# Two mixers of a two-block network: sixteen of their twenty-eight weight blocks multiplied in float32 straight from the loaded blocks

## The chip, the cores and the metric

The kernel runs on one core of one Trainium2 chip. A core has five engines with a program each: TensorE (PE in the profile, with its weight loads as PEld), VectorE (DVE), ScalarE (ACT), GpSimd (POOL) and SyncE (SP), which here issues the loads. The metric is the device time of one execution in microseconds (us), as the median of several runs; less is better.

## The reference, cut to what matters

A sequence of 256 tokens with 1024 features goes through two blocks of two layers each, everything in float32. The first block (attention, RWKV time mixing, two convolution FFNs) is not touched. Each layer of the second block begins with a mixer:

```python
def second_block(x, c, positions, ...):
    for l in range(DEPTH):                       # DEPTH = 2
        mod = jax.nn.silu(c) @ ada_w[l] + ada_b[l]
        sh1, sc1, g1, sh2, sc2, g2 = jnp.split(mod[:, None, :], 6, axis=-1)
        h = rmsnorm(x, ln1_g[l]) * (1.0 + sc1) + sh1
        z = h @ w_in[l]                          # 1024 -> 2560
        xr, yr, q, k, v = jnp.split(z, splits, axis=-1)
        lru = rg_lru(causal_conv(xr, conv_w[l], conv_b[l]), ...) * jax.nn.gelu(yr)
        att = diff_attention(q, k, v, positions, ...)
        x = x + g1 * (jnp.concatenate([lru, att], axis=-1) @ w_out[l])
        h = rmsnorm(x, ln2_g[l]) * (1.0 + sc2) + sh2
        f = swiglu(h, ...) if l % 2 == 0 else moe(h, ...)
        x = x + g2 * f
    return rmsnorm(x, final_g)
```

The attention has four heads, each the difference of two softmaxes of 64-wide queries and keys, followed by an rms norm of the head's output. The recurrence `rg_lru` has 512 channels, a convolution of four taps ahead of it and two gates from small block matrices.

## The kernel before, in words

**Layout and products.** Activations lie feature-major: eight tiles of 128 features x 256 tokens. All large weights are packed on the host into blocks of 128 x 1024 floats (512 KB) in the order of use. A block is either *split* or *raw*. For a split block ScalarE casts it to fp32r (`whi`, line 377) and VectorE or GpSimd subtracts that from the raw block (`wlo`, line 379). The activations have such parts too, `Ahi` and `Alo`. A product is then three fp32r matmuls, hi x hi, lo x hi and hi x lo (`mm3`, lines 595 to 597; token-major, for the values, lines 624 to 626). A raw block is multiplied as it is in float32; before the change only the first block of the network has such blocks.

**The stream.** `Stream` keeps two free lists, of raw buffers and of pairs for split blocks. `advance` issues loads on SyncE as long as there is a raw buffer, and splits as long as there is a pair; a split gives its raw buffer back when both parts are made, and a pair is free again when the next block is taken. In the first mixer there are ten raw buffers and five pairs, in the second fourteen and four. `k.st.share = 3` makes every third split of a mixer a GpSimd one, and splits are then given a priority of 60 over other work.

**A mixer** is `mixer2`, run with l = 0 and l = 1. Its steps are written in one list, `MIX_ORDER`:

```python
MIX_ORDER = "q0 x0 s0 q1 x1 s1 q2 v0 s2 t0 q3 v1 m0 s3 r0 n0 t1 y0 m1 t2 m2 n1 y1 t3 o0 n2 m3 o1 n3 o2 l0 l1 o3 l2 l3".split()
```

q (queries and keys of a head), x (the recurrence's input), v (values) and y (gate) take two blocks each, o and l (output rows for a head and for four feature tiles of the recurrence) one each: 28 blocks. s is scores and softmax, t the transposes of the softmax, m its product with the values, n the head's norm, r the recurrence. q0 and x0 run ahead of the norm's factors by token (`start`, results scaled by the row `frow`; `scaled`, line 1504, writes them to `gy` and `th`). After x0, `norm_split` makes the normed input for everything else: for each feature tile a product on VectorE (`nt`, line 573), `Ahi` on ScalarE (574) and `Alo` on VectorE (575). For l = 0 the residual h, which is still the result of the first block before its last norm, is multiplied by that norm's row and gain on GpSimd, two products for each of eight tiles (1544 and 1545). The row lies in the tile of the values, `V`.

The names that the steps use: `xc` the convolution (three products on VectorE for each feature tile, line 1562), `gates` its matmuls (1567), `rope_in`, `rope_sw` and `rope_out` the rotation of queries and keys (675, 683 to 685), `sc` the scores (1594, maximum 695, exponential 701, scaling 1597 to 1601), scores' matmuls 1592, transposes 1609 to `PT`, product with the values 1618, `sq` a square for the statistics (499, matmul 459), `rs` the factors by token (542, on GpSimd).

**What sets the order.** The program is written step by step as in the list, and a scheduler then orders each engine's instructions by priority (place in the program, less the bonus of the splits) and its own estimate of when their inputs are there. On the chip each engine takes its instructions strictly in that order.

**The stretches.** Mixer 1 has a start (q0, x0, with the residual of the layer before) to 818.4 us, a middle (the other sixteen blocks of q, x, v and y) from 818.4 to 902.1 and an out stage (o and l) to 927.2; then follows the FFN. Mixer 2 has them up to 1153.3, 1237.7 and 1262.8, then the routing and the experts to the end.

Of the kernel before, what the change touches and what calls it, by code (L numbers as in the profile page):

```python
# [10 lines left out]
F32 = mybir.dt.float32  # L11
# [3 lines left out]
AF = mybir.ActivationFunctionType  # L15
# [4 lines left out]
P = 128  # L20
T = 256
# [13 lines left out]
# ---------------------------------------------------------------- layout  # L35
# [53 lines left out]
def _const_arrays():  # L89
# [11 lines left out]
    # up to here for the first block only  # L101
# [19 lines left out]
def _colunit(w, c0, n=256):  # L121
    """columns c0:c0+n of a [1024, *] matrix as [128, 8*n], rows of one partition d = kt*128 + p"""
    return w[:, c0:c0 + n].reshape(-1, P, n).transpose(1, 0, 2).reshape(P, -1)


# steps of a mixer of block 2: queries and keys, scores, turned scores, values and output of the heads (q, s, t, m, o),
# the projections of values, recurrence and gate (v, x, y), the recurrence (r) and its output (l)
# [4 lines left out]
# the tokens and two more columns  # L132
# [7 lines left out]
def stream_units(inp):  # L140
    """blocks [128, 1024] of the streamed weights in the order of use; with inp None only their number"""
# [68 lines left out]
    for l in range(2):  # L210
        for c in MIX_ORDER:
            n, i = c[0], int(c[1:])
            if n == "q":
                add(2048, lambda: _colunit(np.concatenate([win[l][:, 1024 + i * P:1024 + (i + 1) * P], win[l][:, 1536 + i * P:1536 + (i + 1) * P]], 1), 0))
            elif n in MIX_COLS:
                add(2048, lambda: _colunit(win[l], MIX_COLS[n] + 256 * i))
# [57 lines left out]
class K:  # L274
    """state shared by the stages"""
# [15 lines left out]
# ---------------------------------------------------------------- weight stream  # L291
class Stream:
    """weights in the order of use: loads run ahead, then hi and lo parts but for the raw ones"""

    def __init__(self, k):
# [3 lines left out]
        # free memory for loads and for parts: what always stays, and what stays to the end of some phases  # L299
# [14 lines left out]
    def open(self, raw, spl, phases=1):  # L314
        """for the next phases: blocks to load and split blocks on top of those that stay"""
# [7 lines left out]
    def extend(self, more, upto=1):  # L323
        """more blocks to load, to the last one or up to one"""
# [35 lines left out]
    def _cuts(self, n):  # L360
        """the last blocks go in halves"""
# [27 lines left out]
    def after(self, n):  # L389
        """what follows on ScalarE comes after the split of the n-th block from here"""  # L390
        return self.k.tc.issue_after(self.ins[min(self.cur + n, self.nsplit - 1)])

    def done(self):
        """the parts handed out last are used"""
# [4 lines left out]
    def get(self):  # L399
        """the next block: its parts, or a raw one, kept until free()"""  # L400
# [10 lines left out]
    def free(self):  # L411
# [1723 lines left out]
```

## Time and profile before

| what | value |
|---|---|
| time, median of three runs | 2157.73 us (2155.24 to 2157.91) |
| span of the profiled execution | 2161.8 us |
| TensorE busy | 2060.4 us, 95% |
| VectorE busy | 1808.6 us, 84% |
| ScalarE busy | 1361.7 us, 63% |
| GpSimd busy | 302.8 us, 14% |
| two mixers, start to end of the out stages | 798.4 to 927.2 and 1137.2 to 1262.8 |

The span is that of one execution, taken by the profiler; it lies 4.1 us above the median of the runs. The busy time of a pipelined TensorE does not say that it is at its peak: the distance from one matmul's start to the next does, and so does the clock that the throttle granted, which the windows give as a share of 2.4 GHz (0.50 is 1.2 GHz). A float32 matmul shows as two records. A row of the waits says which instruction of another engine ended TensorE's idle time.

### The profile page before, as it was taken

To read this page: it belongs to the slowest core of one execution; us is meant where nothing else is said; L and a number is where in the kernel's file an instruction comes from. 1 tells how busy PE (TensorE), PEld (TensorE's weight loads), DVE (VectorE), ACT (ScalarE), POOL (GpSimd) and SP (SyncE) were. 2 spreads that over 40 slices of the span, in tenths; PEclk is the share of its full clock that TensorE was granted. 3 is DMA by queue.
4 is the path that set the end of the run, shared out by engine and by line. 5 is a ranking of instruction groups with operands and counts; after the bars stand their busy time and mean duration, and the time that the engine had idled before them with its cause. 6 is when DMAs were issued, how large, how long until landed. Compare 5 with 4: busy or idle time off the path is not lost. (4 is left out here: it accounts for less than half of the span.)

```text
span 2161.8 us, 37324 instructions
## 1 busy us (share of the span) xinstructions
PE 2060.4 (95%) x14240; PEld 1824.0 (84%) x14240; DVE 1808.6 (84%) x2393; ACT 1361.7 (63%) x1923; POOL 302.8 (14%) x246
## 2 busy tenths in 40 slices
PE   8999998888999998899998999999999999999997
PEld 7889997786889997899997878888888878787875
DVE  6879868794479869789979779998999889888987
ACT  6665555663365556554447657777777777777775
POOL 1011117651121114310002220000000000000002
PEclk9999998887999999999999899999999999999999
DMA  7358742221178752378965359998999999999992
GB/s 297 127 176 303 258 138 92 69 89 50 55 272 301 268 181 89 126 266 338 330 220 186 114 213 358 354 348 321 352 366 345 341 347 368 343 339 347 367 345 73
DMA packets 147915, 533.48 MB, mean 247 GB/s; under 512 B 16784, under 2 KB 17040, under 8 KB 147600
## 3 DMA queue, kind: packets, MB, share of 16 engines
q1 hardware_dynamic: 147728, 531.02, 68.0%
q8 instruction: 114, 1.87, 0.3%
q14 instruction: 73, 0.60, 0.1%
HBM read 529.90 MB, written 1.05 MB: 246 GB/s over the span
## 5 line engine op out<-in xcount | busy, mean ns | idle before, releaser
L379 DVE TENSOR_TENSOR wlo<-raw,whi 128x1024 fp32r<-128x1024 f32 (+1 forms) x642 | 782.4, 1235 | 111.1 <-ACT whi L377 109.4
L377 ACT CAST whi<-raw 128x1024 fp32r<-128x1024 f32 (+1 forms) x666 | 684.0, 1041 | 267.8 <-PE acc L596 67.3
L595 PE MATMUL mm<-Ahi,whi 128*128 128x256 f32 (+1 forms) x1208 | 351.1, 291 | 8.2 <-DVE th L1504 4.9
L596 PE MATMUL mm<-Alo,whi 128*128 128x256 f32 (+1 forms) x1208 | 348.9, 289 | 4.0 <-DVE Alo L575 1.9
L597 PE MATMUL mm<-Ahi,wlo 128*128 128x256 f32 (+1 forms) x1208 | 348.3, 289 | 1.8 <-DVE wlo L379 1.8
L1869 PE MATMUL acc<-wlo,XE 128*128 128x512 f32 x768 | 303.9, 396 | 0.8
L1868 PE MATMUL acc<-whi,XE 128*128 128x512 f32 x768 | 304.5, 398 | 0.0
L1870 PE MATMUL acc<-whi,XE 128*128 128x512 f32 x768 | 302.2, 394 | 0.0
L595 PEld LDWEIGHTS mm<-Ahi,whi 128*128 128x128 f32 x1208 | 235.1, 195 | 13.7 <-DVE th L1504 5.3
L596 PEld LDWEIGHTS mm<-Alo,whi 128*128 128x128 f32 x1208 | 235.1, 195 | 6.5 <-DVE Alo L575 2.9
L597 PEld LDWEIGHTS mm<-Ahi,wlo 128*128 128x128 f32 x1208 | 235.4, 195 | 4.8 <-issue 2.5
L379 POOL TENSOR_TENSOR wlo<-raw,whi 128x1024 fp32r<-128x1024 f32 (+1 forms) x24 | 54.5, 2278 | 982.0 <-ACT whi L377 979.3
L379 DVE TENSOR_TENSOR wlo<-more,whi 128x1024 fp32r<-128x1024 f32 x150 | 178.0, 1220 | 10.1 <-ACT whi L377 9.8
L1869 PEld LDWEIGHTS acc<-wlo,XE 128*128 128x128 f32 x768 | 144.3, 188 | 37.9 <-DVE wlo L379 6.8
L377 ACT CAST whi<-more 128x1024 fp32r<-128x1024 f32 x150 | 154.4, 1050 | 34.1 <-PE acc L1870 22.6
L1870 PEld LDWEIGHTS acc<-whi,XE 128*128 128x128 f32 x768 | 144.3, 188 | 33.1
L1868 PEld LDWEIGHTS acc<-whi,XE 128*128 128x128 f32 x768 | 144.3, 188 | 32.1
L596 PE MATMUL acc<-fs,whi 128*128 128x256 f32 x544 | 152.8, 282 | 0.9 <-DVE fs L564 0.8
L597 PE MATMUL acc<-fs,wlo 128*128 128x256 f32 x544 | 152.7, 281 | 0.0
L1902 PE MATMUL mm<-whi,h 128*128 128x512 f32 x384 | 152.1, 396 | 0.0
L595 PE MATMUL acc<-fs,whi 128*128 128x256 f32 x544 | 151.5, 281 | 0.6 <-ACT fs L563 0.5
L1903 PE MATMUL mm<-whi,h 128*128 128x512 f32 x384 | 151.2, 394 | 0.0
(503 smaller groups left out, 4208.0 us busy)
## 6 DMA issues: line engine op xcount, KB each, us to landing
raw<-ws SPq DMA_DIRECT2D x658, 512.0 KB, 5.0
more<-ws SPq DMA_DIRECT2D x150, 512.0 KB, 5.5
adaw<-ada SPq DMA_DIRECT2D x96, 512.0 KB, 5.7
con<-ws SPq DMA_DIRECT2D x27, 512.0 KB, 5.1
tables<-ws SPq DMA_DIRECT2D x26, 512.0 KB, 5.4
rows<-ws SPq DMA_DIRECT2D x25, 512.0 KB, 5.5
XE<-ws SPq DMA_DIRECT2D x10, 512.0 KB, 5.5
raw<-ws SPq DMA_DIRECT2D x12, 256.0 KB, 5.1
```

The lines of the kernel that those rows point to most:

```text
L377: self.ins[n] = nc.scalar.copy(hi[:, s], raw[:, s]).ins
L379: self.last = eng.tensor_tensor(lo[:, s], raw[:, s], hi[:, s].bitcast(F32), op=OP.subtract).ins
L595: nc.tensor.matmul(out, w[0], x[0], start=start, stop=False, **kw)
L596: nc.tensor.matmul(out, w[0], x[1], start=False, stop=False, **kw)
L597: nc.tensor.matmul(out, w[1], x[0], start=False, stop=stop, **kw)
L1868: nc.tensor.matmul(ps, xe[0][:, kt], w[0], start=(kt == 0), stop=False)
L1869: nc.tensor.matmul(ps, xe[0][:, kt], w[1], start=False, stop=False)
L1870: nc.tensor.matmul(ps, xe[1][:, kt], w[0], start=False, stop=(kt == KT - 1))
L1902: nc.tensor.matmul(py[e][q], x[0][i], w[0][i], start=(c == 0 and f + i == 0), stop=False)
L1903: nc.tensor.matmul(py[e][q], x[1][i], w[0][i], start=False, stop=False)
```

## The change

1. Sixteen blocks of each mixer (q1 to q3, x1, v0, v1, y0, y1) are marked raw. The new `proj32` multiplies them in float32, eight matmuls for a block, and gives each block back by itself as soon as its products are written (`free(u)`). q0, x0, o and l stay split.
2. Their operand is one float32 tile `x32` (a tile of the group "Ahi"). `norm_split` becomes `norm`: a product on VectorE and an addition on ScalarE for each tile, no low part.
3. `share` and with it the splits' priority are not set any more: no split of a mixer is on GpSimd.
4. For l = 0 the residual's scaling is a step of its own, `normed`, after y0 in the program: one product with both factors for each tile, on VectorE. The row has a tile of its own.

Comments and docstrings are gone too; so line numbers of after differ by up to some twenty. The diff, cut to its core:

```diff
@@ stream_units @@
+            ahead = c in ("q0", "x0")
             if n == "q":
-                add(2048, lambda: ...)
+                add(2048, lambda: ..., raw=not ahead)
             elif n in MIX_COLS:
-                add(2048, lambda: _colunit(win[l], MIX_COLS[n] + 256 * i))
+                add(2048, lambda: _colunit(win[l], MIX_COLS[n] + 256 * i), raw=not ahead)
@@ class Stream @@
-    def free(self):
+    def free(self, block=None):
         for c, t in self.held:
-            self.free_raw[c].append((c, t))
-        self.held = []
+            if block is None or t is block:
+                self.free_raw[c].append((c, t))
+        self.held = [] if block is None else [x for x in self.held if x[1] is not block]
@@ norm_split @@
-def norm_split(k, A, h, g, sh, row):
-    nc = k.nc
-    hi, lo = A
+def norm(k, x, h, g, sh, row):
     for kt in range(KT):
         t = k.pn.tile([P, T], F32, name="nt", bufs=3)
-        nc.vector.scalar_tensor_tensor(t, h[:, kt], g(kt), row, op0=OP.mult, op1=OP.mult)
-        nc.scalar.activation(hi[:, kt], t, AF.Identity, bias=sh(kt))
-        nc.vector.scalar_tensor_tensor(lo[:, kt], t, sh(kt), hi[:, kt].bitcast(F32), op0=OP.add, op1=OP.subtract)
+        k.nc.vector.scalar_tensor_tensor(t, h[:, kt], g(kt), row, op0=OP.mult, op1=OP.mult)
+        k.nc.scalar.activation(x[:, kt], t, AF.Identity, bias=sh(kt))
@@ new @@
+def proj32(k, ps, x, tm=False):
+    for kt in range(KT):
+        if kt % 4 == 0:
+            u = k.st.get()
+        for m in range(2):
+            if tm:
+                l, r = x[:, kt, m * P:(m + 1) * P], u[:, (kt % 4) * 256:(kt % 4 + 1) * 256]
+            else:
+                l, r = u[:, (kt % 4) * 256 + m * P:(kt % 4) * 256 + (m + 1) * P], x[:, kt]
+            k.nc.tensor.matmul(ps[:, m * T:(m + 1) * T], l, r, start=(kt == 0 and m == 0), stop=(kt == KT - 1), skip_group_check=True)
+        if kt % 4 == 3:
+            k.st.free(u)
@@ mixer2 @@
-        frow, row = V[:, 0, :TW], V[:, 1, :T]
+        frow = V[:, 0, :TW]
+        row = pool.tile([P, T], F32, name="row") if l == 0 else None
...
-            f(k, ps, A1)
+            proj32(k, ps, x32[0], tm)
...
-            norm_split(k, A1, h, lambda kt: g1[:, kt:kt + 1], col(0), frow[:, :T])
-            if l == 0:
-                for kt in range(KT):
-                    nc.gpsimd.tensor_tensor(h[:, kt], h[:, kt], row, op=OP.mult)
-                    nc.gpsimd.tensor_tensor(h[:, kt], h[:, kt], k.V("nfin", kt).to_broadcast([P, T]), op=OP.mult)
+            x32.append(part(k, "Ahi", F32)[:, :, :T])
+            norm(k, x32[0], h, lambda kt: g1[:, kt:kt + 1], col(0), frow[:, :T])
+        def normed():
+            for kt in range(KT):
+                nc.vector.scalar_tensor_tensor(h[:, kt], h[:, kt], k.V("nfin", kt), row, op0=OP.mult, op1=OP.mult)
...
-        k.st.share = 3
         for c in MIX_ORDER:
             steps["step_" + c[0]](int(c[1:]))
+            if l == 0 and c == "y0":
+                normed()
...
-        k.st.share = 0
```

How the order of the engines moves, at three places. Rows give line, operation, output<-inputs and shape, x with the number in a row; numbers behind a name tell buffers apart.

TensorE in mixer 1 before, right behind x0's last product (`acc` and `mm` are banks of results, `whi_90` and so on the parts of a block):

```order
L595 MATMUL acc<-Ahi,whi_94 128x258
L596 MATMUL acc<-Alo,whi_94 128x258
L597 MATMUL acc<-Ahi,wlo_95 128x258
L595 MATMUL mm<-Ahi,whi_90 128x256
L595 MATMUL mm<-Ahi,whi_6505 128x256
L596 MATMUL mm<-Alo,whi_90 128x256
L597 MATMUL mm<-Ahi,wlo_91 128x256
```

The triples go on up to the first gates' matmuls, 88 matmuls in all. TensorE in mixer 1 after, at the same place (`raw_...` are raw buffers):

```order
L595 MATMUL acc<-Alo,whi_94 128x258
L596 MATMUL acc<-Ahi,wlo_95 128x258
L640 MATMUL mm<-Ahi,raw_6503 128x256 x8
L640 MATMUL mm<-Ahi,raw_6504 128x256 x6
L1586 MATMUL acc<-xc,gates 128x256 x4
L1611 MATMUL acc<-rope_out 128x256 x4
L640 MATMUL mm<-Ahi,raw_6504 128x256 x2
L640 MATMUL mm<-Ahi,raw_89 128x256 x8
L640 MATMUL mm<-Ahi,raw_86 128x256 x8
L640 MATMUL mm<-Ahi,raw_88 128x256 x6
L1586 MATMUL acc<-xc,gates 128x256 x2
```

The runs of threes are runs of float32 matmuls with a block's buffer as one side, and the gates and scores of the first heads stand after fourteen of them.

GpSimd in mixer 1 before, from the FFN ahead of it (`fg`) to the residual's scaling:

```order
L825 TENSOR_TENSOR fg<-fx,fg 128x256 x22
L379 TENSOR_TENSOR wlo_91<-raw_6503,whi_90 128x1024
L542 TENSOR_TENSOR rs_8979<-ms_8976,mh 128x4
L379 TENSOR_TENSOR wlo_6508<-raw_86,whi_6507 128x1024
L1544 TENSOR_TENSOR h<-h,V_8870 128x256 x2
L1545 TENSOR_TENSOR h<-h,vec 128x256 x2
```

GpSimd after, from the same place:

```order
L839 TENSOR_TENSOR fg<-fx,fg 128x256 x22
L544 TENSOR_TENSOR rs_8974<-ms_8971,mh 128x4
L544 TENSOR_TENSOR rs_9427<-ms_9425,mh 128x2
L1673 TENSOR_TENSOR gy<-gy,xc 128x256 x2
L544 TENSOR_TENSOR rs_9505<-ms_9503,mh 128x2
```

The splits and the sixteen products of the residual have left; the factors of the norms and the products of gate and recurrence stay.

VectorE in mixer 1 before, near the rotation for head 3 and its scores:

```order
L379 TENSOR_TENSOR wlo_95<-raw_88,whi_94 128x1024
L675 COPY rope_sw<-rope_in 32x512 x2
L683 TENSOR_TENSOR rope_out<-rope_in,tables 128x512
L684 TENSOR_TENSOR rope_sw<-rope_sw,tables 128x512
L379 TENSOR_TENSOR wlo_93<-raw_87,whi_92 128x1024
L685 TENSOR_TENSOR rope_out<-rope_out,rope_sw 128x512
```

VectorE after, from the end of the recurrence (`xc<-ra,ri`) and the scores of head 2, in two pieces:

```order
L1613 SCALAR_TENSOR_TENSOR sc_9290<-acc,tables 128x512
L709 TENSOR_REDUCE mx_9304<-sc_9302 128x2
L709 TENSOR_REDUCE mx_9292<-sc_9290 128x2
L380 TENSOR_TENSOR wlo_6508<-raw_87,whi_6507 128x1024
L717 RECIPROCAL rc_9297<-sm_9294 128x2
```

The second link stands right behind head 2's two maxima. Some seven rows further on in the same order, at the end of the next rotation:

```order
L699 TENSOR_TENSOR rope_out<-rope_out,rope_sw 128x512
L380 TENSOR_TENSOR wlo_91<-raw_87,whi_90 128x1024
L539 TENSOR_SCALAR ms_9425<-tp 128x2
L380 TENSOR_TENSOR wlo_93<-raw_87,whi_92 128x1024
L1613 SCALAR_TENSOR_TENSOR sc_9388<-acc,tables 128x512
L1613 SCALAR_TENSOR_TENSOR sc_9400<-acc,tables 128x512
```

The splits that stay, for o and l, take their turns through one raw buffer, `raw_87`, where consecutive splits had different buffers before; a first one stands right ahead of the two rows of scores above.

## Rows read from the trace of the kernel before

**Rows 1.** Windows: us, busy time (instructions) of each engine, TensorE clock, DMA share, GB/s.
```profile
798.40:818.40 20.00, 18.23 (x166) 16.46 (x165) 12.40 (x24) 11.12 (x23) 5.03 (x3) 0.91 0.32 106
818.40:902.10 83.70, 70.42 (x491) 63.68 (x489) 76.80 (x124) 55.69 (x105) 30.98 (x27) 0.88 0.32 107
...
902.10:927.20 25.10, 24.99 (x212) 24.48 (x209) 15.55 (x18) 12.66 (x21) 9.13 (x6) 1.00 0.45 148
...
1153.30:1237.70 84.40, 74.07 (x537) 67.39 (x536) 74.20 (x125) 57.49 (x109) 19.31 (x11) 0.88 0.34 113
...
1300.00:2100.00 800.00, 799.23 (x3619) 644.08 (x3618) 725.49 (x710) 605.35 (x661) 0.00 (x0) 1.00 0.94 349
```

**Rows 2.** TensorE's waits (us, times, longest), 818.4 to 902.1, then 1153.3 to 1237.7.
```profile
PE mm L595 <- DVE th L1504: 3.0, 1, 3.0
PE acc L1592 <- DVE rope_out L685: 2.1, 1, 2.1
PE mm L596 <- DVE Alo L575: 1.9, 2, 1.6
PE tp L459 <- ACT sq L499: 1.8, 1, 1.8
...
PE acc L1592 <- DVE rope_out L685: 5.2, 1, 5.2
PE mm L595 <- DVE th L1504: 1.9, 1, 1.9
```

**Rows 3.** Windows over the six slices of the middles at half clock.
```profile
820.97:827.79 6.82, 5.81 (x25) 5.52 (x26) 6.79 (x11) 5.07 (x10) 5.91 (x7) 0.50 0.13 49
...
sum 40.95, PE 35.18 PEld 31.02 DVE 35.08 ACT 20.51 POOL 8.38; mean PE 5.86 PEld 5.17 DVE 5.85 ACT 3.42 POOL 1.40
```

**Rows 4.** TensorE timeline (start, us, instruction, count); last, L1618's group (busy us, mean ns).
```profile
849.79 0.28 PE L596 MATMUL mm<-Alo,whi 128*128 128x256 f32 x1
849.91 0.28 PE L597 MATMUL mm<-Ahi,wlo 128*128 128x256 f32 x1
...
874.14 1.02 PE L1618 MATMUL tp<-PT,V 128*128 128x256 f32 x4
...
L1618 PE MATMUL tp<-PT,V 128*128 128x256 f32 x32 | 8.3, 382 | 0.4 <-ACT PT L1611 0.4
```

**Rows 5.** Timelines of VectorE (first and last) and GpSimd, around 1209 and 843.
```profile
1209.37 2.91 DVE L675 COPY rope_sw<-rope_in 32x512 f32<-32x512 f32 x2
...
1209.38 2.61 POOL L379 TENSOR_TENSOR wlo<-raw,whi 128x1024 fp32r<-128x1024 f32 x1 [9.96 <-ACT whi L377]
...
842.78 0.85 DVE L675 COPY rope_sw<-rope_in 32x512 f32<-32x512 f32 x2
```

**Rows 6.** VectorE's groups, 818 to 897: busy us, mean ns, idle before.
```profile
L379 DVE TENSOR_TENSOR wlo<-raw,whi 128x1024 fp32r<-128x1024 f32 x10 | 12.6, 1257 | 0.3 <-ACT whi L377 0.3
...
L575 DVE SCALAR_TENSOR_TENSOR Alo<-nt,mod,Ahi 128x256 fp32r<-128x256 f32 x8 | 6.5, 863 | 0.0
L573 DVE SCALAR_TENSOR_TENSOR nt<-h,g,V 128x256 f32<-128x256 f32 x7 | 6.5, 966 | 0.0
L1594 DVE SCALAR_TENSOR_TENSOR sc<-acc,tables 128x512 f32<-128x512 f32 x8 | 5.5, 684 | 2.4 <-PE acc L1592 2.1 <-PE tp L1609 0.3
```

**Rows 7.** ScalarE's groups, 818 to 897.
```profile
L377 ACT CAST whi<-raw 128x1024 fp32r<-128x1024 f32 x16 | 16.5, 1040 | 5.7 <-PE mm L596 4.3 <-POOL h L1544 1.2 <-issue 0.2
...
L574 ACT ACTIVATE Ahi<-nt,mod 128x256 fp32r<-128x256 f32 x8 | 3.8, 504 | 3.7 <-DVE nt L573 3.7
```

**Rows 8.** DMA issues (count, KB, median us to landing): 820 to 900, then the page.
```profile
raw<-ws SPq DMA_DIRECT2D x16, 512.0 KB, 3.4
...
raw<-ws SPq DMA_DIRECT2D x658, 512.0 KB, 5.0
```

**Rows 9.** TensorE's waits by releaser, 798.4 to 818.4.
```profile
PE mm L596 <- DVE Alo L589: 1.2, 1, 1.2
```

**Rows 10.** The page's first line on the span.
```profile
span 2161.8 us, 37324 instructions
```

More of the change, by code (lines that the diff above doesn't have):

```diff
@@ L212, in stream_units @@
             n, i = c[0], int(c[1:])
+            ahead = c in ("q0", "x0")
             if n == "q":
-                add(2048, lambda: _colunit(np.concatenate([win[l][:, 1024 + i * P:1024 + (i + 1) * P], win[l][:, 1536 + i * P:1536 + (i + 1) * P]], 1), 0))
+                add(2048, lambda: _colunit(np.concatenate([win[l][:, 1024 + i * P:1024 + (i + 1) * P], win[l][:, 1536 + i * P:1536 + (i + 1) * P]], 1), 0), raw=not ahead)
             elif n in MIX_COLS:
-                add(2048, lambda: _colunit(win[l], MIX_COLS[n] + 256 * i))
+                add(2048, lambda: _colunit(win[l], MIX_COLS[n] + 256 * i), raw=not ahead)
             elif n in MIX_ROWS:
@@ L1515, in mixer2, with proj @@
         acc = []
-        def proj(f):
+        x32 = []
+        def proj(tm=False):
             ps = psum(k, "mm")
-            f(k, ps, A1)
+            proj32(k, ps, x32[0], tm)
             return ps.rearrange("p (a t) -> p a t", a=2)
@@ L1540, in start @@
             S["x"].append(scaled(pb, th))
-            norm_split(k, A1, h, lambda kt: g1[:, kt:kt + 1], col(0), frow[:, :T])
-            if l == 0:
-                for kt in range(KT):
-                    nc.gpsimd.tensor_tensor(h[:, kt], h[:, kt], row, op=OP.mult)
-                    nc.gpsimd.tensor_tensor(h[:, kt], h[:, kt], k.V("nfin", kt).to_broadcast([P, T]), op=OP.mult)
-                k.dump("x_b1", h)
+            x32.append(part(k, "Ahi", F32)[:, :, :T])
[3 more added lines that the diff above has]
+                nc.vector.scalar_tensor_tensor(h[:, kt], h[:, kt], k.V("nfin", kt), row, op0=OP.mult, op1=OP.mult)
+            k.dump("x_b1", h)
         def out(x):
@@ L1553, in step_x @@
         def step_x(j):
-            ps = S["x"].pop(0) if S["x"] else proj(proj_fm)
+            ps = S["x"].pop(0) if S["x"] else proj()
             for m in range(2):
@@ L1572, in step_v @@
         def step_v(j):
-            ps = proj(proj_tm)
+            ps = proj(tm=True)
             nc.scalar.copy(V[:, :, j * 256:(j + 1) * 256], ps)
@@ L1580, in step_q @@
             else:
-                x = rope_in(k, pool, proj(proj_fm).rearrange("p a t -> p (a t)"))
+                x = rope_in(k, pool, proj().rearrange("p a t -> p (a t)"))
             S["q"][hd] = rope(k, pool, *x, k.cos2, k.sin2)
@@ L1649, in step_y @@
         def step_y(j):
-            ps = proj(proj_fm)
+            ps = proj()
             nc.scalar.activation(gy[:, 2 * j:2 * j + 2], ps, AF.Gelu_apprx_tanh)
```

## The prediction

> **What bounds the kernel now.** I read the stages first: a table of windows with each engine's busy time and the granted clock [rows 1]. It falls apart cleanly. The out stage of a mixer (902.1 to 927.2) and the experts (1300 to 2100) have TensorE busy from end to end at full clock. The two middles, where the sixteen blocks of the change are multiplied, do not: 83.7 us with TensorE busy 70.4 at a mean clock of 0.88, and 84.4 us with 74.1, again at 0.88. Idle time and clock are therefore all that the change can win, and only there and in the short start ahead of the first middle (0.91).
>
> The idle part of a middle is in the table of TensorE's waits by releaser [rows 2]: 13.0 us in the first (ten entries, the largest four shown; the rest are rope_in 1.4, issue 0.8, rc 0.7, sc 0.6, PT 0.4, Ahi 0.3), 10.0 us in the second (five, the largest two shown; the rest sc 1.3, xc 1.2, ACT's sc 0.4). The releasers are VectorE and ScalarE, nearly always. In the first middle VectorE is busy 76.8 of 83.7 us: it is what TensorE waits for. The clock part is in three cold slices of each middle, at half clock [rows 3] (one slice stands there, and the sum of the six). Half of TensorE's busy time in them is lost, 35.18/2 = 17.6 us: 8.2 in the first middle (16.35 busy), 9.4 in the second (18.83). They lie where TensorE has pauses: the first begins within the 3.0 us wait for th. So the work of a middle at full clock is 70.4 - 8.2 = 62.2 us and 74.1 - 9.4 = 64.7 us.
>
> **The products: longer.** A block is 24 fp32r matmuls now. They start 0.12 us apart [rows 4], from 849.79 to 849.91, and over the run of 42 that these two end 0.119, so a block is 24 x 0.119 = 2.86 us and three matmuls are 0.357. After it, a block is 8 float32 matmuls of the same 128 x 256. The trace counts two records for such a matmul. At full clock the group of four records, two matmuls, at 874.14 lasts 1.02 us [rows 4]; one record lasts 0.38 (the mean of L1618's group), which leaves (1.02 - 0.38)/3 = 0.213 from start to start, 0.43 a matmul. From above, 1.02/2 = 0.51 with the drain of the pipeline counted in. From below, the three fp32r matmuls that it replaces, 0.357, if the stream were bound by something other than the array. A middle has 128 such matmuls: 128 x (0.43 - 0.357) = +9.3 us, between 0 and +19.6. I take 0.43: in runs of eight to forty matmuls the drain is met rarely, and the 0.213 is a start-to-start time of just this shape and type.
>
> The Trainium skill (FP8 and Floating Point Precision, "TensorE Precision Notes") says that true FP32 takes four passes through the array. With passes as long as the fp32r matmuls of this stream that is, as an estimate, 4 x 0.119 = 0.476 a matmul and 5.9 us more in each middle than my term; the row at 874.14 is below that, and the measurement decides.
>
> **VectorE, ScalarE and GpSimd: less.** What goes: sixteen splits of a middle (an ACT cast of 1.04 us each and a subtraction, 1.26 us on VectorE or 2.61 on GpSimd) and the eight low parts of the normed input, 6.5 us [rows 5 to 7]. What comes: eight products of the residual on VectorE in mixer 1, priced at the norm's own product of the same form, 0.97 us with what disturbed it, some 5 to 8 us. GpSimd's splits, nine in and around the first middle and six around the second, also hold VectorE: two copies to rope_sw take 0.85 us alone and 2.91 while a split runs on GpSimd [rows 5], so 2.1 us a collision; with no splits there this is gone. GpSimd keeps only the small powers and gy's products (the piece of its order shows that the sixteen residual rows are gone too). VectorE in middle 1 then has 76.8 - 12.6 - 6.5 + 8 or less, under 66 of some 81 us, and in middle 2 still less: it no longer bounds the stage, but chains through it still do.
>
> **What waits remain.** Middle 1, by the list [rows 2]: th 3.0 becomes 0.7, since the first raw products need only one norm tile (product 0.97, ACT 0.50, partly beside x0's last matmuls) instead of tile, low part and scaled rows; Alo 1.9, Ahi 0.3 and rope_in 1.4 (a copy behind ACT's casts) go; rope_out 2.1 stays, since between s1 and s2 VectorE's rows of the new order, at the durations of before, add to some 11 us and TensorE's to 9.9; sq 1.8, sc 0.6, PT 0.4 are chains untouched; issue and rc 1.5 become 1.0. Left 6.6. Middle 2: rope_out 5.2 loses a collision (2.1) and a split (1.2), left 1.9; th 0.7; sc 1.3; ACT's sc 0.4; xc 1.2 goes with the split ahead of it. Left 4.3. What is late next is in VectorE's order: the splits for o and l are now a chain through one buffer, raw_87. A link is the load's landing 3.4, ACT 1.04 and VectorE 1.26 and 0.2 of issue, 5.9 us [rows 6 to 8]; between the first two links stand two rows like L1594 and two reductions as long, 4 x 0.68 = 2.7 us. VectorE, in order, then idles 3.2 us, and behind the split wait head 2's softmax and TensorE's transposes. TensorE has raw blocks to multiply meanwhile, so I allow 1 us in each middle. All the bounds: from 2.2 us left (sq and PT alone) to the whole 13.0 and 10.0.
>
> **Clock.** With about half the pauses, I keep one cold slice of 3.4 us in each middle, 1.7 us lost, between none and the 8.2 and 9.4 now.
>
> **Elsewhere.** In mixer 1's start TensorE waits 1.2 us for a low part [rows 9] that VectorE makes while a GpSimd split runs, and the clock of 0.91 costs 0.09 x 20 = 1.8 us [rows 1]. The split goes. The gain lies between 0 and 3.0; I take half, -1.5. The out stages are TensorE's own in before and after: 0. The FFN between is untouched. The experts: TensorE busy 799.23 of 800, DMA 0.94; a shift of the second mixer passes to the end, unless loads set it (a rival).
>
> **Sum.** Middle 1: 62.2 + 9.3 + 6.6 + 1.0 + 1.7 = 80.8, against 83.7: -2.9. Middle 2: 64.7 + 9.3 + 4.3 + 1.0 + 1.7 = 81.0, against 84.4: -3.4. Start -1.5. Together -7.8 us on the profiled span of 2161.8 [rows 10]: 2154.0. That span is 4.1 above the median of the runs, so **2149.9 us**.
>
> **The rivals.** (a) *The cold slices stay*. The clock falls after pauses, and three chains still make TensorE pause where it does now: th, rope_out, the head's statistics. Then 8.2 and 9.4 are lost as before, +6.5 and +7.7 on the sum: 2149.9 + 14.2 = 2164.1. It decides when waits and clock together lose more than 11.9 and 10.1 us of the 21.2 and 19.4 lost now, which is what +9.3 leaves of them. For it: three slices lie in each middle though their waits differ. Against: the largest waits shrink. (b) *The chain through raw_87 meets TensorE*. With the page's landing of 5.0 [rows 8] a link is 7.5 us and VectorE idles 4.8 between the first two; met in full in both mixers this is 2 x (4.8 - 1.0) = +7.6: 2157.5. For it: in the piece of VectorE's order the third and fourth links stand with one small row between them. Against: only rows for heads 2 and 3 stand behind it, and l blocks give TensorE work. (c) *Nearly all waits go*: only 2.2 and 0.4 stay, and no cold slice. 62.2 + 9.3 + 2.2 = 73.7 and 64.7 + 9.3 + 0.4 = 74.4, each -10.0, start -1.5: 2136.2. For it: VectorE falls by a fifth and ACT by 16.5 of 55.7 us. (d) *Four passes at the pace of this stream*, 0.476 a matmul: 2 x 5.9 = +11.8: 2161.7; the upper bound, 0.51, would be 2170.4. The row at 874.14 is against it. The Trainium skill's section named above states the four passes. (e) *The experts' loads take back the second mixer's gain*: the DMA share is 0.94 there, and a first block that waits for its load would not come sooner. +3.4: 2153.3. Against: TensorE is busy all but 0.8 of 800 us. That the change does not do what it says is out: the orders show the float32 runs, and GpSimd without splits.
>
> **How the numbers follow.** Forecast 0.42 (its own range 2144 to 2156: waits 3 us more or less in each middle), (a) 0.13, (b) 0.14, (c) 0.20, (d) 0.05, (e) 0.06. A measurement of this kernel can tell about 0.2%, 4.3 us, from no change: faster is under 2153.4, slower over 2162.0. Faster: 0.36 of the forecast, 0.19 of (c), 0.03 of (e), 0.02 of (b), 0.60. Slower: 0.12 of (a), 0.02 of (d), 0.01 of (b), 0.15. The rest, 0.25, is the same. The range leaves out (a) and the outer edge of (c): 2135 to 2162.
>
> **What would show it.** Float32 runs in the middles with records 0.213 to 0.22 apart and blocks of 3.44 us; VectorE's th and Alo gone from TensorE's waits; copies to rope_sw near 0.42 each; at most one slice at half clock in a middle; a middle of 81 us. The forecast is wrong if the records are 0.24 or more apart, if 0.88 stays as the clock, or if VectorE waits for whi of raw_87 with TensorE waiting behind it.

## The result, and the profile after

The changed kernel takes 2138.64 us (median of four runs, 2136.51 to 2142.05), the kernel before 2157.82 us on the same chip. The ratio is 0.9898 with a 95% interval of 0.9881 to 0.9915: 1.0% or 19.2 us faster. The forecast was 2149.9, inside a range of 2135 to 2162; the sign was right and the gain 2.4 times as large as forecast. The time is within 2.5 us of rival (c), nearly all waits gone (2136.2, chance 0.20).

In the profiled executions the gain is 24.2 us (2161.8 to 2137.6), somewhat more than between the medians, since the profiled span before lay 4.1 us above its median and the one after 1.0 below. The windows of the changed kernel, cut at the same places as [rows 1], show where it is (us, busy time and instructions of each engine, TensorE clock, DMA share, GB/s): start, middle and out stage of mixer 1, then start and middle of mixer 2, then the experts.

```profile
798.13:815.18 17.05, 16.45 (x167) 14.99 (x165) 9.27 (x27) 8.83 (x22) 1.01 (x1) 1.00 0.10 32
815.18:888.05 72.87, 71.35 (x360) 59.47 (x361) 53.26 (x113) 44.22 (x92) 3.86 (x5) 1.00 0.43 145
888.05:912.78 24.73, 24.73 (x211) 24.42 (x210) 11.90 (x18) 10.97 (x18) 2.12 (x3) 1.00 0.45 150
...
1122.85:1138.63 15.78, 14.38 (x125) 12.95 (x123) 11.86 (x27) 9.20 (x22) 4.78 (x6) 1.00 0.62 235
1138.63:1214.58 75.95, 74.36 (x409) 62.38 (x409) 49.66 (x105) 45.01 (x95) 3.61 (x5) 1.00 0.42 139
...
1300.00:2100.00 800.00, 799.17 (x3621) 644.00 (x3620) 723.69 (x709) 603.70 (x659) 0.00 (x0) 1.00 0.94 345
```

Start 1 went from 20.0 to 17.1 us, middle 1 from 83.7 to 72.9, middle 2 from 84.4 to 76.0; the out stages are 0.3 shorter each, and the routing between the second mixer and the experts is 1.2 shorter. There TensorE waits less for `sel`, a tile of VectorE (first row before, second row after):

```profile
PE acc L1767 <- DVE sel L1764: 4.4, 1, 4.4
...
PE acc L1786 <- DVE sel L1783: 2.6, 1, 2.6
```

This too goes with GpSimd's splits: the wait is 4.4 us in all three kernels of this document in which GpSimd has splits of a mixer, and 2.6 in all the others, also where the products stay fp32r. The experts run as before, so the gain of the second mixer reached the end. In both middles TensorE is busy for all but 1.5 and 1.6 us, and its clock is 1.00: the slices at half clock of [rows 3] are all gone. What TensorE still waits for (us in total, times, longest), in mixer 1 and then in mixer 2 from the start to the end of its middle:

```profile
PE acc L1611 <- ACT V L1593: 1.5, 1, 1.5
PE mm L640 <- ACT Ahi L574: 0.6, 1, 0.6
...
PE acc L1611 <- DVE rope_out L699: 1.6, 1, 1.6
PE mm L595 <- DVE Alo L588: 0.6, 1, 0.6
PE mm L640 <- ACT Ahi L574: 0.6, 1, 0.6
```

These are the lists of [rows 2] after: th, sq, the middle's low parts and the rest do not stand in them any more. (The rows of 0.6 us lie in the starts or end them, so that 1.5 and 1.6 are left for the middles.)

The float32 runs, in TensorE's timeline (start, us, instruction, records):

```profile
850.93 1.14 PE L1611 MATMUL acc<-rope_out 64*128 64x256 f32 x8 [1.49 <-ACT V L1593]
852.00 0.66 PE L1628 MATMUL tp<-ident,sc 128*128 128x128 f32 x4
852.49 7.07 PE L640 MATMUL mm<-Ahi,raw 128*128 128x256 f32 x32
```

Thirty-two records, sixteen matmuls or two blocks, in 7.07 us; with a last record of 0.38 as in [rows 4] that is (7.07 - 0.38)/31 = 0.216 from start to start, 0.432 a matmul.

### The profile page after: what moved, and what is told of

Same layout as the page of the kernel before. It is cut to its first block, busy times and chain, and to the rows that moved or that the text cites. A ratio compares the mean times of both kernels' runs of the same rounds, so it can differ in the third digit from the quotient of the medians.

```text
span 2137.6 us, 36646 instructions
## 1 busy us (share of the span) xinstructions
PE 2059.8 (96%) x13984; PEld 1813.3 (85%) x13984; DVE 1749.3 (82%) x2372; ACT 1330.7 (62%) x1891; POOL 234.8 (11%) x211
## 4 chain that ended last, share of the span: by engine, by line
PE 53%; DVE 2%; ACT 1%; issue 0%; DMA 0%; POOL 0%; ACTq 0%; POOLq 0%; DVEq 0%
PE acc L1888 8%; PE acc L1889 8%; PE acc L1887 8%; PE mm L1921 4%; PE mm L1922 4%; PE mm L1924 4%; PE mm L640 2%; PE acc L595 2%; PE acc L596 1%; PE acc L594 1%; PE mm L596 1%; PE mm L595 1%; PE mm L594 1%; PE tp L596 1%; PE tp L595 1%; PE tp L594 1%
## 5 line engine op out<-in xcount | busy, mean ns | idle before, releaser
L380 DVE TENSOR_TENSOR wlo<-raw,whi 128x1024 fp32r<-128x1024 f32 x629 | 765.5, 1234 | 117.6 <-ACT whi L378 115.2
L378 ACT CAST whi<-raw 128x1024 fp32r<-128x1024 f32 (+1 forms) x635 | 650.6, 1041 | 262.2 <-PE acc L595 69.4
L594 PE MATMUL mm<-Ahi,whi 128*128 128x256 f32 (+1 forms) x1016 | 290.8, 286 | 1.8 <-ACT whi L378 1.7
L596 PE MATMUL mm<-Ahi,wlo 128*128 128x256 f32 (+1 forms) x1016 | 288.7, 284 | 1.7 <-DVE wlo L380 1.7
L595 PE MATMUL mm<-Alo,whi 128*128 128x256 f32 (+1 forms) x1016 | 288.6, 284 | 0.7 <-DVE Alo L588 0.6
L594 PEld LDWEIGHTS mm<-Ahi,whi 128*128 128x128 f32 x1016 | 193.8, 191 | 4.8 <-issue 2.0
L596 PEld LDWEIGHTS mm<-Ahi,wlo 128*128 128x128 f32 x1016 | 193.8, 191 | 3.9 <-DVE wlo L380 2.1
L595 PEld LDWEIGHTS mm<-Alo,whi 128*128 128x128 f32 x1016 | 193.6, 191 | 2.1 <-DVE Alo L588 1.1
L898 DVE SCALAR_TENSOR_TENSOR adaw<-adaw,adac 128x1024 f32<-128x1024 f32 x96 | 122.0, 1273 | 14.4 <-DMA adaw<-ada 14.0
```

The costliest lines, as they stand in the source:

```text
L378: self.ins[n] = nc.scalar.copy(hi[:, s], raw[:, s]).ins
L380: self.last = eng.tensor_tensor(lo[:, s], raw[:, s], hi[:, s].bitcast(F32), op=OP.subtract).ins
L594: nc.tensor.matmul(out, w[0], x[0], start=start, stop=False, **kw)
L595: nc.tensor.matmul(out, w[0], x[1], start=False, stop=False, **kw)
L596: nc.tensor.matmul(out, w[1], x[0], start=False, stop=stop, **kw)
L898: nc.vector.scalar_tensor_tensor(x, x, 1.0, c, op0=OP.mult, op1=OP.mult, accum_out=raw[:, j:j + 1])
```

## The experiments

Two questions were open. Nearly all waits went, not half: which part of the change did that? And is the float32 product, which makes TensorE's own work longer, a part of the gain or a price paid out of it? Each run was timed beside the kernel before on the same chip (2161.87, 2162.15 and 2159.93 us in the three sets); times below are medians, ratios are to that. "Start, middle and out" are the stages of [rows 1]. Their lengths tell small differences better than the medians do: the six stages (start, middle and out of both mixers) of the changed kernel add to 231.1 and 231.5 us in two profiled executions, while the first mixer began 2.0 us apart in the two, behind a first block that the change doesn't touch. Before, the six add to 254.4.

**Without GpSimd's splits.** The first theory, Q, is one half of the prediction's account: VectorE and ScalarE have too much split work. Its rival, G: GpSimd holds VectorE. This is the kernel before with one line changed:

```diff
-            eng = nc.gpsimd if self.share and n % self.share == 0 else nc.vector
+            eng = nc.vector
```

> The kernel before with every split of the mixers on VectorE; priority of the splits, fp32r products and the residual on GpSimd stay. Theory Q (queues): what made TensorE pause was the amount of split work that stands ahead of the small rows on VectorE and ScalarE; the eight splits or so of a mixer that GpSimd made then cost VectorE 1.26 us each, 10 us more, and take away some collisions of 2.1 us. Expected: middles of 80 to 88 us, clock still below 0.95, time between 4 us faster and 6 us slower than before. Theory G (GpSimd): it was GpSimd that held VectorE; then both middles lose most of their waits, under 77 us each, and the time falls by 12 us or more.

Measured: 2142.06 us, ratio 0.9906 (0.9876 to 0.9935). VectorE got all the splits, and the kernel became 20 us faster, as much as by the whole change. Its middles:

```profile
821.21:896.79 75.58, 65.05 (x460) 59.40 (x459) 70.63 (x123) 52.80 (x98) 13.95 (x18) 0.93 0.33 110
...
1153.34:1220.01 66.67, 63.37 (x487) 58.95 (x487) 62.71 (x120) 53.05 (x99) 3.74 (x4) 0.97 0.37 122
```

VectorE is busy for less time than before although it has more to do: 98.3 and 93.0 us over start, middle and out of the two mixers, against 104.7 and 101.3. It makes ten and nine splits more in them, 12.1 and 11.3 us, so all its other instructions together take 18.5 and 19.7 us less: 2.0 us for each split that left GpSimd. The out stages took 3 us more. Theory Q falls for this part. The residual still runs on GpSimd here, and that can be told apart in VectorE's groups (mean ns behind the busy time; 821 to 897):

```profile
L575 DVE SCALAR_TENSOR_TENSOR Alo<-nt,mod,Ahi 128x256 fp32r<-128x256 f32 x8 | 6.8, 885 | 0.0
L573 DVE SCALAR_TENSOR_TENSOR nt<-h,g,V 128x256 f32<-128x256 f32 x7 | 4.7, 711 | 0.0
L1601 DVE SCALAR_TENSOR_TENSOR sc<-sc,rc,sc 128x256 f32<-128x256 f32 x8 | 3.5, 479 | 0.0
```

The scores, at 1016 before, are back at 479; the norm's rows, which run beside the residual's products, are not.

**The rest of the change without the raw blocks.** The kernel before, with no GpSimd splits, no priority and the residual on VectorE; products and low parts stay fp32r:

```diff
...
-            if l == 0:
-                for kt in range(KT):
-                    nc.gpsimd.tensor_tensor(h[:, kt], h[:, kt], row, op=OP.mult)
-                    nc.gpsimd.tensor_tensor(h[:, kt], h[:, kt], k.V("nfin", kt).to_broadcast([P, T]), op=OP.mult)
...
+        def normed():
+            for kt in range(KT):
+                nc.vector.scalar_tensor_tensor(h[:, kt], h[:, kt], k.V("nfin", kt), row, op0=OP.mult, op1=OP.mult)
...
-        k.st.share = 3
...
+            if l == 0 and c == "y0":
+                normed()
...
```

> The kernel before with everything of the change but the raw blocks: no GpSimd splits, no priority, the residual's scaling on VectorE after y0; products and low parts stay fp32r. Theory Q: VectorE has all split work and eight products more; middles of 80 to 90 us, time within 6 us of before to either side. Theory G: 12 us or more faster, most of the change's 19 us.

Measured: 2131.05 us, ratio 0.9863 (0.9836 to 0.9890); faster than the whole change. Repeated later (below): 2134.34, ratio 0.9877 (0.9860 to 0.9894). Its six stages add to 224.5 us in both profiled executions. Its windows, start, middle and out of mixer 1, then the middle of mixer 2:

```profile
796.74:813.77 17.03, 16.51 (x167) 15.04 (x165) 11.99 (x27) 11.61 (x24) 1.01 (x1) 1.00 0.39 125
813.77:883.20 69.43, 62.80 (x487) 57.30 (x485) 67.25 (x131) 54.02 (x103) 4.19 (x4) 1.00 0.36 116
883.20:910.47 27.27, 25.33 (x215) 24.82 (x213) 16.39 (x25) 12.57 (x20) 4.01 (x4) 1.00 0.50 171
...
1137.04:1206.51 69.47, 66.29 (x537) 60.49 (x537) 66.88 (x128) 56.12 (x107) 5.52 (x5) 1.00 0.40 135
```

This is the price of float32 as measured: TensorE at clock 1.00 is busy 62.80 us in middle 1 with fp32r and 71.35 with float32, 66.29 and 74.36 in middle 2, 8.6 and 8.1 us more. Over all six stages the raw blocks win more than half of that back: 231.1 and 231.5 us with them against 224.5 without are 6.6 and 7.0 more. What they win is waits: TensorE is idle for 6.6 and 3.2 us in these two middles and for 1.5 and 1.6 in the changed kernel's, and the first out stage is 2.5 shorter there. And why the clock and the waits are better at the same split work is in VectorE's groups of this kernel, to be held against [rows 6] (mean ns behind the busy time):

```profile
L575 DVE SCALAR_TENSOR_TENSOR Alo<-nt,mod,Ahi 128x256 fp32r<-128x256 f32 x8 | 3.5, 480 | 0.0
L1602 DVE SCALAR_TENSOR_TENSOR sc<-sc,rc,sc 128x256 f32<-128x256 f32 x8 | 3.5, 478 | 0.0
L573 DVE SCALAR_TENSOR_TENSOR nt<-h,g,V 128x256 f32<-128x256 f32 x7 | 3.0, 478 | 0.0
```

The same instructions had means of 863 (Alo) and 966 (nt) before, and the scores' 1016:

```profile
L1601 DVE SCALAR_TENSOR_TENSOR sc<-sc,rc,sc 128x256 f32<-128x256 f32 x8 | 7.8, 1016 | 0.0
```

By the run before this one, the scores were held by GpSimd's splits, the low parts by the residual, and nt by both. One place in the kernel before shows how such a mean comes about, GpSimd's and VectorE's timelines at 876:

```profile
876.16 2.52 POOL L379 TENSOR_TENSOR wlo<-raw,whi 128x1024 fp32r<-128x1024 f32 x1 [8.48 <-ACT whi L377]
...
876.36 3.00 DVE L1601 SCALAR_TENSOR_TENSOR sc<-sc,rc,sc 128x256 f32<-128x256 f32 x2
```

Two instructions of 0.48 take 3.00 us, as long as GpSimd's split lasts and one instruction more. So this GpSimd split took some 2.1 us from VectorE, as [rows 5] show for a copy, and what it relieved VectorE of was 1.26. Most splits do so: beside sixteen of the nineteen GpSimd splits of the two mixers stands one VectorE instruction that lasts 2.3 to 2.7 us and takes 0.2 to 0.5 alone.

**The raw blocks alone.** The changed kernel, with GpSimd doing what it did before:

```diff
             norm(k, x32[0], h, lambda kt: g1[:, kt:kt + 1], col(0), frow[:, :T])
+            if l == 0:
+                for kt in range(KT):
+                    nc.gpsimd.tensor_tensor(h[:, kt], h[:, kt], row, op=OP.mult)
+                    nc.gpsimd.tensor_tensor(h[:, kt], h[:, kt], k.V("nfin", kt).to_broadcast([P, T]), op=OP.mult)
...
+        k.st.share = 3
         for c in MIX_ORDER:
             steps["step_" + c[0]](int(c[1:]))
-            if l == 0 and c == "y0":
-                normed()
...
```

> The changed kernel with GpSimd as it was before: every third of the splits that are left (o, l) with their priority, and the residual's sixteen products, on GpSimd. Raw blocks alone. Theory Q: nearly all of the gain stays; the middle of mixer 1 is 73 to 76 us, time 0 to 4 us above the changed kernel. Theory G: the middles are 80 us or more with clock below 0.95, and at least half of the 19 us is lost.

Measured: 2151.39 us, ratio 0.9950 (0.9934 to 0.9965). Half of the gain is gone, as theory G has it. The middles are back at 80 us with cold slices:

```profile
812.52:893.33 80.81, 73.44 (x360) 60.33 (x361) 55.70 (x106) 44.32 (x92) 17.25 (x20) 0.98 0.38 130
...
1144.17:1224.49 80.32, 77.18 (x408) 64.33 (x409) 50.30 (x104) 45.15 (x95) 5.96 (x6) 0.96 0.38 132
```

Three things came back together, the residual, every third split of those left, and the splits' priority. In mixer 1 the residual alone does nearly all of it (a run below: 79.9 us). In mixer 2's middle only one split is GpSimd's, and the wait of 3.1 us for rope_out stands behind rows of the recurrence and a split on VectorE that were put into that rotation; whether the hold or the priority made this middle longer is not told apart.

**The load of the split work put back.** The changed kernel; in mixer 1 alone each raw block is also cast and subtracted, and the norm makes its low parts, into memory that nobody reads:

```diff
+            nc.scalar.copy(dhi, raw)
+            for s in (slice(0, W // 2), slice(W // 2, W)):
+                nc.vector.tensor_tensor(dlo, raw[:, s], dhi[:, s], op=OP.subtract)
...
+            k.nc.vector.scalar_tensor_tensor(lo[:, kt], t, sh(kt), x[:, kt], op0=OP.add, op1=OP.subtract)
```

> The changed kernel with the load of the removed split work put back in mixer 1 alone: for each of its sixteen raw blocks a cast on ScalarE and two subtractions of 512 columns on VectorE, and the eight low parts of the norm, all into memory that nobody reads. TensorE's float32 products wait for none of it; mixer 2 is as in the changed kernel. Theory Q: middle 1 is back at 79 to 86 us, with VectorE busy 75 us, waits for rope_out, th and scores again and slices at half clock; 6 to 13 us slower than the changed kernel. Theory F (the float32 runs themselves, longer for each block, cover the small chains): middle 1 stays at 73 to 76 us with clock 1.00, time within 3 us of the changed kernel.

Measured: 2144.38 us, ratio 0.9923 (0.9896 to 0.9949), some 5 us above the changed kernel, all of it in middle 1 (79.5 us; mixer 2 as in the changed kernel, 75.8). Window and TensorE's waits:

```profile
818.02:897.49 79.47, 73.44 (x361) 59.76 (x361) 71.19 (x149) 55.93 (x105) 4.11 (x5) 0.98 0.40 133
```

```profile
PE tp L564 <- POOL rs L549: 2.5, 1, 2.5
PE acc L1593 <- DVE xc L1588: 1.7, 2, 1.5
PE tp L466 <- ACT sq L506: 0.9, 1, 0.9
```

So theory Q holds too, as the smaller of two effects: 18 us more on VectorE and 12 on ScalarE are 6.6 us more of the middle. The rival, theory F, that float32 runs cover the chains by their length, falls: its 73 to 76 us were not met.

**Priority and residual apart.** Three more kernels split the second part of the change; the changed kernel went with them. First the kernel before without the priority alone:

```diff
-            with self.k.tc.high_priority(offset=60) if self.share else ExitStack():
+            with ExitStack():
```

> The kernel before without the priority of the splits; every third split of the mixers and the residual stay on GpSimd. The last four runs left open which part of GpSimd's work and of the order it was. Theory L (lock): VectorE is held while GpSimd runs a split, whenever it runs; middles of 80 to 86 us with half-clock slices, within 6 us of before. Theory P (priority): splits pushed ahead of the small rows were the larger cost; then 8 to 15 us faster than before though GpSimd still splits.

Measured: 2167.85 us, ratio 1.0027 (1.0011 to 1.0043): slightly slower. Theory P falls. Theory L has the time, but not middle 1, 90.4 us where it allowed 86; middle 2 is 81.8, 2.7 shorter than before. Then before without splits on GpSimd and without priority, the residual left on GpSimd:

```diff
-        k.st.share = 3
```

> The kernel before without GpSimd splits and without the priority; the residual's sixteen products stay on GpSimd (that part alone is what this run adds to the run of the whole rest of the change, 1.37% faster than before). If the residual on GpSimd matters, middle 1 is 74 us or more against 69.4 there, mixer 2 as there (69.5), time 5 to 10 us above that run: 20 us faster than before. If it doesn't, 28 to 31 us faster.

Measured: 2133.64 us, ratio 0.9874 (0.9840 to 0.9907). Middle 1 is 73.6 us with the clock at 0.95, mixer 2 nearly as without the residual (70.6). That is 28.5 us faster than before, the time expected if the residual did not matter, with a middle just short of the 74 us expected if it did. Against the two runs of the whole rest the medians do not settle it (30.8 and 25.6 us faster than before). By mixer 1's three stages the residual cost 1.6 us (115.4 against 113.7): the middle became 4.1 longer and the out stage 2.5 shorter. Between this kernel and the first experiment (2142.06) lie the priorities alone: 8.4 us by the medians, 6.7 by the six stages. While GpSimd splits, the priority helps by 5.7, all of it in mixer 1; without GpSimd's splits it hurts. That the splits then stand ahead of small rows that TensorE waits for is a likely reason, which no run shows by itself.

```profile
820.29:910.67 90.38, 74.41 (x490) 67.11 (x489) 77.09 (x122) 55.00 (x104) 31.08 (x27) 0.85 0.27 91
```

```profile
812.64:886.21 73.57, 66.03 (x490) 60.08 (x489) 72.10 (x128) 54.55 (x104) 17.11 (x21) 0.95 0.34 110
```

The first row is middle 1 without the priority, the second without GpSimd splits and priority. Then the changed kernel with the residual on GpSimd (the first piece of the diff of the raw blocks alone, and `normed` gone, without `share`):

> The changed kernel with the residual's scaling on GpSimd as before, right behind the norm; no GpSimd splits, no priority. If the sixteen products hold VectorE and so TensorE, the middle of mixer 1 is 77 to 81 us (72.9 in the changed kernel, 80.8 with all of GpSimd's work back) and mixer 2 stays at 76; time 4 to 8 us above the changed kernel. If they don't, 72 to 75 us and no difference above 2 us.

Measured: 2144.60 us, ratio 0.9924 (0.9904 to 0.9944), against 2140.23 of the changed kernel in the same set. Middle 1 is 79.9 us, seven more, mixer 2 unchanged (76.4). The place is seen in the timelines, GpSimd's residual, VectorE's convolution and the gates' matmuls on TensorE that wait for it:

```profile
821.06 0.90 POOL L1562 TENSOR_TENSOR h<-h,row 128x256 f32<-128x256 f32 x1
...
820.55 4.57 DVE L1586 SCALAR_TENSOR_TENSOR xc<-th,vec,xc 128x255 f32<-128x255 f32 x6
...
824.06 3.25 PE L1591 MATMUL acc<-xc,gates 128*128 128x256 f32 x8 [3.91 <-issue]
```

Six products of the convolution take 4.57 us, where six of 0.48 overlap to some 2.6, TensorE stands 3.9 us ahead of the gates, and a cold slice follows. ("issue" is named because the releaser is not in the records; the fourth of the six products, the last that the first gates need, ends at 823.85, just ahead of them.) This run shows the hold by itself: the residual's result is not read before the end of the out stage (915.5), VectorE keeps its order from the norm to the convolution, with the residual's own products taken out of it, and still middle 1 is 7.0 us longer. And the changed kernel itself:

> The changed kernel as it is, on the same chip as the three others, so that each can be compared with it and not with the kernel before alone: 0.9881 to 0.9915 of before, middles of 73 and 76 us with clock 1.00.

Measured: 2140.23 us, ratio 0.9897 (0.9865 to 0.9929); middles of 72.9 and 76.3 us. It repeats.

**GpSimd work that nobody waits for.** The changed kernel with sixteen subtractions of 512 columns on GpSimd in the middle of mixer 1, written to unused memory:

```diff
+            if l == 0 and c in ("q1", "x1", "q2", "v0", "q3", "v1", "y0", "y1"):
...
+                for _ in range(2):
+                    nc.gpsimd.tensor_tensor(dump, src, src, op=OP.subtract)
```

> The changed kernel with sixteen GpSimd subtractions of 512 columns put into the middle of mixer 1, two after each of eight steps, into memory that nobody reads; no instruction of VectorE, ScalarE or TensorE waits for them, mixer 2 is untouched. Theory L (GpSimd holds VectorE while both run): VectorE instructions beside them last as long as the GpSimd one, the sum of VectorE's busy time in middle 1 rises by 8 to 20 us though it has no instruction more, middle 1 goes from 72.9 to 75 us or more, time 2 to 8 us above the changed kernel. Theory S (what cost the time before was waiting for the slow splits themselves): VectorE's busy time stays at 53 us and middle 1 at 73.

Measured: 2145.59 us, ratio 0.9938 (0.9917 to 0.9959), 5 us above the changed kernel; middle 1 is 80.2 us. Time and middle are as theory L has it, and theory S, with 53 and 73 us, falls. But VectorE's busy time rose by 2.4 us only (55.7), not 8 to 20, and the 7 us come from one wait, 5.0 us for rope_out, with some 3.7 us lost to the half clock behind it. Part of that wait is order: the scheduler put recurrence rows and a split into that rotation. The hold itself is there, but small:

```profile
863.84 2.61 POOL L1687 TENSOR_TENSOR dump<-V 128x512 bf16<-128x512 f32 x2 [11.13 <-ACT V L1593]
...
864.02 1.53 DVE L698 TENSOR_TENSOR rope_sw<-rope_sw,tables 128x512 f32<-128x512 f32 x1
865.48 1.52 DVE L1666 TENSOR_TENSOR_SCAN xc<-ra,ri 128x256 f32<-128x256 f32 x1
```

The rotation's product takes 1.53 us where it takes 0.69 alone, the scan 1.52 for 0.66. So this run, too, shows the hold without any data dependence, and not how much of the 5 us it made. Why VectorE's time rose so little is in the timelines: most of the sixteen subtractions ran beside rows of scores and their maxima, which kept their usual 0.67 to 0.69 us, or beside nothing.

**Can the better kernel be improved?** The kernel of the rest of the change still waits at the end of middle 1 and in its out stage for the heads' statistics (1.4 us) and factors (3.1). Priority for those steps:

```diff
-            steps["step_" + c[0]](int(c[1:]))
+            with k.tc.high_priority(offset=60) if c[0] in "mn" else ExitStack():
+                steps["step_" + c[0]](int(c[1:]))
```

> The kernel before with the rest of the change (no raw blocks), and a priority of 60 for the steps of a head's output and norm, which TensorE waits for at the end of its middle 1 (1.4 for the statistics' product, 3.1 for the factors of GpSimd in two waits). If these chains were late by their place in the order, 1 to 4 us of the 4.5 go: 2127 to 2131. If they are as short as the chain allows, nothing or a new wait beside: 2130 to 2134.

> The kernel before with the rest of the change but no raw blocks, once more, with more rounds: 0.983 to 0.989 of before, against 0.9897 of the changed kernel. What is told apart is the sign of the raw blocks: float32 costs TensorE 8 to 9 us more a middle and saves at most the 6.6, 1.9 and 3.2 us of waits that this kernel still has, so it should be some 6 to 12 us below the changed kernel.

Measured: 2132.54 us (ratio 0.9880, 0.9859 to 0.9900) with the priority and 2134.34 (0.9877, 0.9860 to 0.9894) without, in the same set: no difference clear of noise. Mixer 1 gained 0.8 us by its three stages and mixer 2 lost 1.8. The repeat lies 5.9 us under the changed kernel's repeat of the set before, on the same chip, with no overlap (2132.16 to 2135.17 against 2138.81 to 2141.66), where 6 to 12 were expected. The stages, 224.5 us in this repeat against 231.5, give 7.0. That is the net price of the raw blocks.

## Why the prediction was right, and where it was not

Put together, by the sum of the six stages, 254.4 us before: GpSimd's splits to VectorE -20.4, the priority dropped -6.7 more, the residual to VectorE -2.8 more (1.6 of it in mixer 1, where the residual is), which is 224.5; and then the raw blocks +6.6 to +7.0, which is the changed kernel. By the medians the raw blocks are +5.9 to +9.2. The same parts in another order give other numbers: with GpSimd's share, priority and residual kept, the raw blocks are worth -10.5, since they also take most of its splits away from GpSimd.

- **The products** (+9.3 a middle at 0.43 a matmul): right. Measured +8.6 and +8.1, which over 128 matmuls is 0.42, and 0.432 in a dense run. The work of a middle at full clock was to be 62.2 + 9.3 = 71.5 and 64.7 + 9.3 = 74.0; it is 71.35 and 74.36. That it fits this well is in part luck: the kernel without raw blocks has 62.80 and 66.29 at clock 1.00, so the work was put 0.6 and 1.6 too low and the product term 0.7 and 1.2 too high. Rival (d) is out. The four passes that the Trainium skill states (FP8 and Floating Point Precision, "TensorE Precision Notes") gave, at 0.119 a pass, the estimate of 0.476 a matmul; these runs show 0.42 to 0.43.
- **What waits remain** (6.6 + 1.0 and 4.3 + 1.0): this is the term that was mis-sized. Left are 1.5 and 1.6. I went through the list of waits and asked of each whether the change touches its own chain; rope_out, sq and sc stayed because theirs was "untouched". But nearly all those chains run through VectorE, and VectorE was late for a reason they have in common: instructions of 0.48 us that took 0.9 to 1.0 in the mean, beside GpSimd's splits and beside its residual. The rows were there [rows 6: nt at 966, Alo at 863], and I used them as prices of VectorE's work, and a collision as 2.1 us in one wait, instead of as time that would come back. VectorE came out at "under 66" for the middle; it is 53.3. The rows that stay (nt, sc<-sc,rc,sc, xc<-th,vec,xc and rc<-rc,nlam) took some 12 us less for the same number. Two errors of that sum cancel in part: five splits for o and l stay on VectorE in the middle, where all ten of the window were taken away, and the residual's products took 3.7 us and not 8. With GpSimd released and all split work kept, 6.6 and 3.2 us of idle time are left; the raw blocks took another 5.1 and 1.6.
- **Clock** (one cold slice left in each, 1.7): none is left. Pauses of up to 1.6 us stood in the changed kernel without a half clock behind them; with 3.1, 3.9 and 5.0 us one followed, in three of the experiments. The kernel of the rest of the change, without raw blocks, has 1.00 in both middles, too.
- **Start** (-1.5): measured -3.0, the upper bound. The wait for the low part [rows 9] and the lower clock both went.
- **The chain through raw_87**, rival (b): it stands in the order, and VectorE waits there, 2.0 us at the most; TensorE does not meet it. The allowance of 1.0 was not needed.
- **Rival (a)**, cold slices as before: it did not come for the changed kernel. **(e)**: the experts passed the gain on.
- **The reason.** The forecast credited the raw blocks and GpSimd's release together. That was wrong as to the first: by itself the removal of split work is worth less than float32 costs. The larger part that the changed kernel won is the release of VectorE from GpSimd. So the time came out in the range, near rival (c) and not near the forecast, and the part that gives the change its name would by itself, with GpSimd already released, have made the kernel slower.

That VectorE is held by GpSimd is a rule of the Trainium skill too (SBUF — State Buffer, "Who interferes with whom"): a VectorE instruction with two SBUF inputs contends with a GpSimd instruction that reads SBUF, and the one that is second is blocked. The traces agree: sc<-sc,rc,sc and nt<-h,g,V were stretched (means of 1016 and 966 ns, 478 without GpSimd's work), while six rows of scores read from a PSUM bank beside GpSimd's unused subtractions took 0.68 to 0.69, as alone. Two inputs are not the whole of it: a copy with one was held as well [rows 5]. What the change shows beyond the rule is the bill: a split given to GpSimd to save VectorE 1.26 us cost it about 2.0 in the mean.

What stays open: how the 20 us of the first experiment divide between VectorE's holds and the later arrival of the slow splits themselves, since the run that was to tell these apart also moved VectorE's order (the residual's run shows that holds alone can cost a middle 7 us, for other GpSimd work); how much of mixer 2's loss in the run of the raw blocks alone comes from the priority; and why the priority hurts once GpSimd has no splits.

## What to carry to other kernels

Before work is moved to GpSimd, compare the mean duration of VectorE's short two-input instructions in that stretch with their duration elsewhere: if 0.48 has become 0.9, the help may cost more than it gives, as here, and every chain through VectorE is late, not only the one that the list of waits names. When a change bundles parts, time the parts: here the part that gave the change its name cost some 7 us of what the others won. A priority is tuned to the durations around it, and has to be tried again when they change (by the medians 5.7 us better with GpSimd's splits, 8.4 worse without).

## What the runs showed of the hardware

A GpSimd split of 2.4 to 2.6 us beside VectorE cost it, in sixteen of nineteen cases, one hold of nearly that length, for one instruction; VectorE's rows around it had their usual 0.48. TensorE's granted clock fell to half around single pauses of 2.5, 3.1, 3.9 and 5.0 us in four middles of the experiments, and stayed at 1.00 through all of both mixers of the changed kernel, whose longest pause is 1.6 (2.0 in its repeat). But the length of a pause alone doesn't tell. In the first experiment, whose longest pause in the middles is 2.1, the clock was 0.93 and 0.97 in them. And in the second mixer a pause of 1.3 us for rope_out stood with a half-clock slice behind it in the kernel without splits and priority, and without one when the residual of the first mixer was on VectorE too. In float32 a matmul of 128 x 128 by 256 columns costs 0.43 us where three fp32r matmuls cost 0.357, so float32 from raw blocks is 20% more time on TensorE, for no split work at all.
